# A hybrid encoder block on one core: the order of the later input projections

## The chip, the cores and the metric

The kernel runs on one core of a Trainium2 chip. The metric is the device time of one execution in microseconds. The core has five engines that each work through a queue of their own: TensorE (PE in the profile; its weight loads are PEld), VectorE (DVE), ScalarE (ACT), GpSimd (POOL) and SyncE (SP), which here only issues DMAs.

## The reference

One layer of an encoder on 1024 tokens of width 1024, all in float32. Both mixers read one input projection:

```python
xn = _rmsnorm(h, norm_mix_w[l])
proj = xn @ w_in[l]                       # columns: q_a, k_a, v_a, qkv_g, z_g, a_g, b_g
attn = _windowed_gqa(q_a, k_a, v_a, ...)  # 8 query heads on 2 key/value heads, window +-128, bias table, sink
gdn  = _gdn_mixer(qkv_g, z_g, a_g, b_g, ...)
h = h + jnp.concatenate([attn, gdn], axis=-1) @ w_out[l]
h = h + jnp.square(jax.nn.relu(_rmsnorm(h, norm_ffn_w[l]) @ w_ffn_in[l])) @ w_ffn_out[l]
return _rmsnorm(h, norm_final_w)
```

The second mixer, a gated delta rule in both directions, works on four heads of width 128. Its q, k and v pass a convolution over 5 tokens and Silu; in chunks it needs the inverse of a triangular matrix (I + A), where A comes from the Gram products of k, and then a scan over the chunks. Its output is normalised and multiplied by Silu(z), the gate.

## The kernel before

Products in full precision are made of three matmuls on a high and a low part of each operand (`mm3`, L124 to L126; the parts come from `split`, a cast on ScalarE, L119, and a subtraction on GpSimd, L120). A product of 128 weight columns with 512 tokens is `gemm`: 8 x 3 matmuls into one PSUM bank of the tag `psA`, of which there are four. `pair` makes four such products from 256 columns, in the order half 0 of both blocks, then half 1 of both; whoever uses `pair` copies each bank out.

Keys and queries of the delta rule are projected first. Then two streams of instructions are woven together by weights. The first is the rest of the input projection: v of the delta rule (`proj_conv`), the gate (`proj_z`), and keys, values and queries of attention (`proj_attn`). The second makes the inverses: `prep` (Gram products per chunk, L631 and L633, decay by Exp on ScalarE, L643, scaling on VectorE, L647 and L655, copies of diagonal blocks, L652, stores to memory `atd` and `pd`), `eliminate` for each direction (31 steps of two VectorE instructions, L675 and L677), `diag_blocks` (VectorE transposes, L686 and L687) and `invert` for the first two of four pairs of chunks (small matmuls L720, L730, L734, L753, L761 with ScalarE copies L714, L723, L744, L755 and memsets on GpSimd, L710, between them). After that, `bias_table` loads four tables of attention's bias (L529), and attention is woven with the other inverses and the scan.

How each projection leaves PSUM:
- v of the delta rule: a ScalarE copy (L394) into a tile of 1028 tokens, on VectorE a scaling (L373) and four multiply-adds (L375) per head, Silu (L377), transposes on PE (L409), a VectorE multiplication (L449) and a store (L450). The tiles and the results lie in buffers of the tag `sc`, of which there are four; `eliminate(1)` and `diag_blocks(1)` use the same tag for their matrices.
- the gate: Silu on ScalarE (L458) and a store `zd` (L459).
- keys and values of attention: a VectorE copy (L476), for keys two DMAs that swap halves, casts and a subtraction; for values a transpose on PE and a copy (L488).
- queries: on VectorE a scaling (L494), on ScalarE a cast (L495), on GpSimd a subtraction (L496), four stores `qad` (L500). `query` (L594) is a DMA on GpSimd's queue that loads a block of queries back. The first two such loads were issued from inside the loop over query products.

The order of the instructions on each engine is set when the kernel is built, by a scheduler that goes by the order in which the code issues them, by buffers that come free, and by its own estimate of times; at run time each engine takes its queue in that order. ScalarE computes Exp and Silu from tables that it loads when the function changes (rows ACT_TABLE_LOAD in the profile).

Of the kernel before, what the change touches and what calls it, by code (L numbers as in the profile page):

```python
# [29 lines left out]
C_AQ, C_AK, C_AV = 0, 512, 640  # L30
C_GQ, C_GK, C_GV, C_Z, C_AB = 768, 1280, 1792, 2304, 2816
# [23 lines left out]
def weave(*streams):  # L55

    live = [[0.0, i, g, w] for i, (g, w) in enumerate(streams)]
    while live:
        s = min(live, key=lambda e: (e[0], e[1]))
        try:  # L60
            v = next(s[2])
            s[0] += v / s[3]
            yield v
        except StopIteration:
            live.remove(s)


def run(gen):
    for _ in gen:
        pass  # L70


def chain(*gens):
    for g in gens:
        yield from g


class Block:
# [380 lines left out]
                nc.sync.dma_start(out=self.zd[2 * p + i, :, half * HALF:(half + 1) * HALF], in_=z)  # L459
                yield 5.2  # L460

    def proj_attn(self):


        nc = self.nc
        w = self.io["w_in"][0]
        raws = self.load_w(self.w_cols(w, C_AK, 256))
        lo, up = slice(0, 64), slice(64, 128)
        self.kh, self.kl = [self.pg(dt=F32R) for _ in range(2)], [self.pg(dt=F32R) for _ in range(2)]
        for v, o in enumerate((up, lo)):  # L470
            nc.vector.tensor_copy(out=self.kl[v][o, :], in_=self.zero[o, :].to_broadcast([64, SEQ]))
        self.va = self.pg((P, NT, P))
        for i, half, ps in self.pair(raws):
            tok = slice(half * HALF, (half + 1) * HALF)
            t = self.pt()
            nc.vector.tensor_copy(out=t, in_=ps)  # L476
            if i == 0:
                swap = self.pt()
                nc.sync.dma_start(out=swap[up, :], in_=t[lo, :])
                nc.sync.dma_start(out=swap[lo, :], in_=t[up, :])  # L480
                for v, (r, o) in enumerate(((lo, up), (up, lo))):
                    nc.scalar.copy(out=self.kh[v][r, tok], in_=t[r, :])
                    nc.scalar.copy(out=self.kh[v][o, tok], in_=swap[o, :])
                    nc.gpsimd.tensor_tensor(out=self.kl[v][r, tok], in0=t[r, :], in1=self.kh[v][r, tok].bitcast(F32),
                                            op=ALU.subtract)
            else:
                pv = self.transposed(t, 0)
                nc.vector.tensor_copy(out=self.va[:, 4 * half:4 * half + 4, :], in_=pv)  # L488
            yield 5.2
        for kv in range(2):  # L490
            raws = self.load_w(self.w_cols(w, C_AQ + 256 * kv, 256))
            for i, half, ps in self.pair(raws):
                q, qh = self.pt(), self.pt(dt=F32R)
                nc.vector.tensor_scalar(out=q, in0=ps, scalar1=0.125, scalar2=None, op0=ALU.mult)  # L494
                nc.scalar.copy(out=qh, in_=q)  # L495
                nc.gpsimd.tensor_tensor(out=q, in0=q, in1=qh.bitcast(F32), op=ALU.subtract)  # L496
                for part, t in enumerate((qh.bitcast(F32), q)):
                    o = 64 * (kv ^ part)
                    for g in range(2):
                        nc.sync.dma_start(out=self.qad[kv, 2 * i + g, o:o + 64, half * HALF:(half + 1) * HALF],  # L500
                                          in_=t[64 * g:64 * g + 64, :])
                if i == 1 and half == 0:
                    self.qs.append(self.query(0, kv))
                yield 5.2


# [747 lines left out]
    def phases(self):  # L1254
        nc = self.nc
        w = self.io["w_in"][0]
# [9 lines left out]
        for half in range(2):  # L1266
# [5 lines left out]
            else:  # L1272
# [11 lines left out]
        tt = [[None] * 4, [None] * 4]  # L1284
        self.ct, self.ctt = [None, None], [None, None]
        self.kc, self.qc = [None] * 4, [None] * 4
        self.qs = []
        self.wo, self.hnt, self.scanned, self.summed, self.rows = [{}, {}], [None, None], set(), [], {}
        run(weave((chain(self.proj_conv(C_GV, "v"), self.proj_z(), self.proj_attn()), 145.0),
                  (chain(self.prep(), self.eliminate(0), self.diag_blocks(0), self.eliminate(1), self.diag_blocks(1),  # L1290
                         self.invert(tt, (0, 1))), 100.0)))
        self.bias_table()

        self.X = {n: [] for n in ("B11", "B21", "B22", "N1", "T2", "T3", "N4")}
        cols, rest = {}, {}
# [82 lines left out]
```

## Time and profile before

| | us |
|---|---|
| median of 3 runs (lowest, highest) | 1255.21 (1253.97, 1259.02) |
| the profiled execution, its own time | 1255.02 |
| its span, from the first to the last instruction | 1253.3 |
| TensorE busy | 1191.6 |
| VectorE busy | 854.9 |
| ScalarE busy | 621.4 |
| GpSimd busy | 580.3 |

The mean granted TensorE clock is 0.983 of full speed. All times of instructions are microseconds from the start of the span. Matmuls overlap in the pipeline, so a row of 0.40 us can follow the one before it after 0.23 us. A row with a bracket shows how long the engine was idle before the instruction and what ended that; the releaser is inferred, and can be a neighbour of the true one. Groups by line show the count, busy us, the mean ns of one, and the idle time before them.

### The profile page before, as it was taken

To read this page: it belongs to the slowest core of one execution; us is meant where nothing else is said; L and a number is where in the kernel's file an instruction comes from. 1 tells how busy PE (TensorE), PEld (TensorE's weight loads), DVE (VectorE), ACT (ScalarE), POOL (GpSimd) and SP (SyncE) were. 2 spreads that over 40 slices of the span, in tenths; PEclk is the share of its full clock that TensorE was granted. 3 is DMA by queue.
4 is the path that set the end of the run, shared out by engine and by line. 5 is a ranking of instruction groups with operands and counts; after the bars stand their busy time and mean duration, and the time that the engine had idled before them with its cause. 6 is when DMAs were issued, how large, how long until landed. Compare 5 with 4: busy or idle time off the path is not lost.

```text
span 1253.3 us, 18527 instructions
## 1 busy us (share of the span) xinstructions
PE 1191.6 (95%) x6482; PEld 967.2 (77%) x6482; DVE 854.9 (68%) x1528; ACT 621.4 (50%) x1347; POOL 580.3 (46%) x488
## 2 busy tenths in 40 slices
PE   7999999899789989998999999999999999999997
PEld 5778777677568868877788888888777888888885
DVE  5667667982389986676655454544668797886976
ACT  6455688335485752125464554545545434444343
POOL 5354211362432433144573534535445665655595
PEclk9999999899889999998999999999999999999999
DMA  7134344441956678122234344443678624434323
GB/s 239 52 121 133 101 171 140 139 126 40 223 168 158 190 216 296 60 84 85 84 131 159 132 151 143 154 159 134 223 280 280 223 85 167 151 121 148 95 90 135
DMA packets 121630, 187.62 MB, mean 150 GB/s; under 512 B 11043, under 2 KB 64416, under 8 KB 121537
## 3 DMA queue, kind: packets, MB, share of 16 engines
q1 hardware_dynamic: 96708, 152.58, 37.9%
q10 hardware_dynamic: 16381, 29.67, 6.3%
q0 software_dynamic: 8448, 4.20, 1.9%
q8 instruction: 51, 0.84, 0.3%
q14 instruction: 42, 0.34, 0.1%
HBM read 122.39 MB, written 63.49 MB: 148 GB/s over the span
## 4 chain that ended last, share of the span: by engine, by line
PE 49%; DVE 6%; DMA 3%; issue 2%; POOL 1%; ACT 1%; ACTq 0%; POOLq 0%; DVEq 0%; SPq 0%
PE psA L124 8%; PE psA L125 8%; PE psA L126 8%; PE psB L126 7%; PE psB L125 7%; PE psB L124 7%; DMA pg<-sd 3%; PE psB L797 2%; DVE pg L1154 1%; DVE pt L1163 1%; DVE wr L1166 1%; PE psB L209 1%; DVE pg L1199 1%; DMA sd<-pt 0%; DVE wr L1161 0%
## 5 line engine op out<-in xcount | busy, mean ns | idle before, releaser
L124 PE MATMUL psA<-pg,wh 128*128 128x512 f32 x416 | 167.6, 404 | 2.1 <-ACT pt L458 2.1
L126 PE MATMUL psA<-pg,wl 128*128 128x512 f32 x416 | 166.9, 401 | 0.0
L125 PE MATMUL psA<-pg,wh 128*128 128x512 f32 x416 | 166.5, 400 | 0.0
L120 POOL TENSOR_TENSOR wl<-wr,wh 128x512 fp32r<-128x512 f32 x44 | 70.2, 1618 | 154.0 <-ACT wh L119 153.9
L1154 DVE TENSOR_TENSOR pg<-pg 128x512 fp32r<-128x512 f32 x112 | 122.7, 1127 | 18.8 <-ACT pg L1153 18.6
L120 POOL TENSOR_TENSOR wh<-wr,wh 128x512 fp32r<-128x512 f32 x32 | 47.9, 1518 | 131.5 <-ACT wh L119 131.5
L1071 ACT ACTIVATE pt<-pt 128x512 f32<-128x512 f32 x64 | 40.4, 632 | 122.7 <-DVE pt L1061 122.7
L125 PE MATMUL psA<-pg,pg 128*128 128x512 f32 x256 | 99.7, 391 | 0.5 <-POOL pg L120 0.5
L124 PE MATMUL psA<-pg,pg 128*128 128x512 f32 x256 | 99.0, 391 | 1.0 <-DVE pg L1199 1.0
L126 PE MATMUL psA<-pg,pg 128*128 128x512 f32 x256 | 99.7, 389 | 0.0
L120 POOL TENSOR_TENSOR pg<-wr,pg 128x512 fp32r<-128x512 f32 x48 | 73.4, 1560 | 51.0 <-ACT pg L119 51.0
L124 PEld LDWEIGHTS psA<-pg,wh 128*128 128x128 f32 x416 | 79.2, 190 | 21.3 <-ACT pt L458 2.4
L125 PEld LDWEIGHTS psA<-pg,wh 128*128 128x128 f32 x416 | 79.3, 191 | 19.7 <-issue 0.9
L126 PEld LDWEIGHTS psA<-pg,wl 128*128 128x128 f32 x416 | 79.1, 190 | 18.6
L1153 ACT CAST pg<-pg 128x512 fp32r<-128x512 f32 x112 | 67.2, 620 | 41.3 <-DMA pg<-sd 31.0
L126 PE MATMUL psB<-pg,pg 128*128 128x512 f32 x192 | 75.0, 390 | 1.3 <-DVE pg L1154 1.3
L125 PE MATMUL psB<-pg,pg 128*128 128x512 f32 x192 | 75.0, 391 | 0.8 <-POOL pg L120 0.7
L124 PE MATMUL psB<-pg,pg 128*128 128x512 f32 x192 | 74.7, 390 | 0.4 <-ACT pg L1153 0.4
L119 ACT CAST wh<-wr 128x512 fp32r<-128x512 f32 x76 | 43.6, 623 | 45.5 <-PE psA L125 24.8
L1061 DVE TENSOR_TENSOR pt<-psB,pt 128x512 f32<-128x512 f32 x39 | 26.9, 689 | 55.1 <-PE psB L126 30.1
L1061 DVE TENSOR_TENSOR pt<-psA,pt 128x512 f32<-128x512 f32 x39 | 26.8, 689 | 55.0 <-PE psA L126 39.5
L124 PEld LDWEIGHTS psA<-pg,pg 128*128 128x128 f32 x256 | 48.0, 188 | 12.6 <-DVE pg L1199 2.3
(385 smaller groups left out, 3307.7 us busy)
## 6 DMA issues: line engine op xcount, KB each, us to landing
sd<-pt ACTq DMA_DIRECT2D x112, 256.0 KB, 2.2
pg<-sd SPq DMA_DIRECT2D x112, 256.0 KB, 2.9
wr<-in_w_ffn_in SPq DMA_DIRECT2D x32, 512.0 KB, 3.8
wr<-in_w_in SPq DMA_DIRECT2D x22, 512.0 KB, 4.8
pg<-in_x SPq DMA_DIRECT2D x16, 512.0 KB, 5.4
wr<-in_w_ffn_out SPq DMA_DIRECT2D x16, 512.0 KB, 4.8
sc<-kvd SPq DMA_DIRECT2D x14, 512.0 KB, 4.1
kvd<-pt SPq DMA_DIRECT2D x16, 256.0 KB, 2.8
```

The source lines that it names most:

```text
L119: nc.scalar.copy(out=h, in_=raw)
L120: (eng or nc.gpsimd).tensor_tensor(out=l, in0=raw, in1=h.bitcast(F32), op=ALU.subtract)
L124: nc.tensor.matmul(ps, wh, xh, start=first, stop=False, skip_group_check=onto)
L125: nc.tensor.matmul(ps, wh, xl, start=False, stop=False, skip_group_check=onto)
L126: nc.tensor.matmul(ps, wl, xh, start=False, stop=last, skip_group_check=onto)
L209: self.nc.tensor.transpose(ps[:, i * P:(i + 1) * P], row[:, k * P:(k + 1) * P], self.ident)
L797: nc.tensor.matmul(ps[:, h - g.start, :], left(h), right[:, h, :], start=True, stop=True)
L1061: self.nc.vector.tensor_tensor(out=out, in0=in0, in1=in1, op=ALU.add)
L1071: self.nc.scalar.activation(out=c, in_=c, func=AF.Relu)
L1153: nc.scalar.copy(out=s[:, 0], in_=raw)
L1154: v.tensor_tensor(out=s[:, 1], in0=raw, in1=s[:, 0].bitcast(F32), op=ALU.subtract)
L1163: v.tensor_tensor(out=b["T2"], in0=b["B22"], in1=b["T1"], op=ALU.subtract)
```

## The change

The first stream is issued in another order: queries of attention, v of the delta rule, keys and values of attention, the gate. For this `proj_attn` is cut into `proj_kv` and `proj_queries`. The first two loads of query blocks leave the loop and follow `bias_table`. No instruction of another kind is added and none is taken out, apart from table loads.

```diff
-    def proj_attn(self):
-
+    def proj_kv(self):
...
             yield 5.2
+
+    def proj_queries(self):
+
+        nc = self.nc
         for kv in range(2):
-            raws = self.load_w(self.w_cols(w, C_AQ + 256 * kv, 256))
+            raws = self.load_w(self.w_cols(self.io["w_in"][0], C_AQ + 256 * kv, 256))
...
-                if i == 1 and half == 0:
-                    self.qs.append(self.query(0, kv))
                 yield 5.2
...
-        self.qs = []
...
-        run(weave((chain(self.proj_conv(C_GV, "v"), self.proj_z(), self.proj_attn()), 145.0),
+        run(weave((chain(self.proj_queries(), self.proj_conv(C_GV, "v"), self.proj_kv(), self.proj_z()), 145.0),
...
         self.bias_table()
+        self.qs = [self.query(0, kv) for kv in range(2)]
```

Lines behind the cut shift by one to three (L476 becomes L475, L488 L487, L494 L497, L496 L499, L500 L503; L631 becomes L632 and so on by one).

VectorE's queue before, at the copy of the first product of values (`psA_2442`, into `pt_2467`): it stands among the steps of the elimination (`sc_2231`, `sc_2233` are the matrices of direction 1, `pg_1921`, `pg_1923` those of direction 0).

```order
L677 TENSOR_TENSOR sc_2233<-sc_2233,pt_2236 128x10x22
L675 TENSOR_TENSOR pt_1926<-pg_1921,pg_1923 128x112
L675 TENSOR_TENSOR pt_2236<-sc_2231,sc_2233 128x207
L677 TENSOR_TENSOR pg_1923<-pg_1923,pt_1926 128x4x28
L476 COPY pt_2467<-psA_2442 128x512
L677 TENSOR_TENSOR sc_2233<-sc_2233,pt_2236 128x9x23
```

The same queue now, at the copies of the first products of keys and values (`psA_2436` keys of half 0, `psA_2490` values of half 0, `psA_2533` keys of half 1). `sc_2238` is the elimination's matrix of direction 1, `sc_2333` and `sc_2396` are the convolved v heads 2 and 3.

```order
L373 TENSOR_SCALAR sc_2333<-sc_2232,cols 128x1024
L678 TENSOR_TENSOR sc_2238<-sc_2238,pt_2241 128x31
L375 SCALAR_TENSOR_TENSOR sc_2333<-sc_2232,cols,sc_2333 128x1024 x4
L373 TENSOR_SCALAR sc_2396<-sc_2277,cols 128x1024
L375 SCALAR_TENSOR_TENSOR sc_2396<-sc_2277,cols,sc_2396 128x1024 x2
L449 TENSOR_TENSOR pt_2345<-psB_2340,irk 128x512
L449 TENSOR_TENSOR pt_2353<-psB_2348,irk 128x512
L687 STREAM_TRANSPOSE sc_2530<-sc_2238 128x1024
L375 SCALAR_TENSOR_TENSOR sc_2396<-sc_2277,cols,sc_2396 128x1024 x2
L688 STREAM_TRANSPOSE sc_2529<-sc_2238 128x1024
L449 TENSOR_TENSOR pt_2408<-psB_2403,irk 128x512
L449 TENSOR_TENSOR pt_2416<-psB_2411,irk 128x512
```

The three copies out of PSUM (`pt_2461`, `pt_2515`, `pt_2558`) come directly behind these rows. They moved from among the elimination's steps to behind its last one (L678, the second row) and behind two convolutions.

TensorE's queue now, where the last product of values (`psA_2683`) ends and the first of the gate (`psA_2764`) begins; before, the first product of queries followed the last product of values directly.

```order
L126 MATMUL psA_2683<-pg_427,wl_2485 128x512
L409 MATMUL psB_2340<-ident,sc_2333 128x128 x4
L409 MATMUL psB_2348<-ident,sc_2333 128x128 x4
L409 MATMUL psB_2403<-ident,sc_2396 128x128 x4
L409 MATMUL psB_2411<-ident,sc_2396 128x128 x4
L124 MATMUL psA_2764<-pg_218,wh_2758 128x512
```

The transposes of v heads 2 and 3 moved in between, and `psA_2764` takes the bank of the fourth product before it, `psA_2436`.

GpSimd's queue before, in the last part of the query products (`pg_2756` and `pg_3229` are tiles that `invert` clears, `pt_2904` and `pt_3096` the first query blocks):

```order
L496 TENSOR_TENSOR pt_2895<-pt_2895,pt_2896 128x512
L594 DMA pt_2904<-qad 128x4x128
L710 MEMSET pg_2756 128x1024
L496 TENSOR_TENSOR pt_2969<-pt_2969,pt_2970 128x512
L496 TENSOR_TENSOR pt_3003<-pt_3003,pt_3004 128x512
L496 TENSOR_TENSOR pt_3047<-pt_3047,pt_3048 128x512
L496 TENSOR_TENSOR pt_3087<-pt_3087,pt_3088 128x512
L594 DMA pt_3096<-qad 128x4x128
L710 MEMSET pg_3229 128x1024
```

And now:

```order
L711 MEMSET pg_2798 128x1024
L711 MEMSET pg_3229 128x1024
L595 DMA pt_3182<-qad 128x4x128
L595 DMA pt_3184<-qad 128x4x128
L595 DMA pt_3221<-qad 128x4x128
```

The loads of query blocks moved behind the memsets of `invert`.

## The prediction

> **What bounds the kernel now.** I read the page first, then the wait list of TensorE, then the timeline and the busy time by stretch around the second half of the input projection, the only part whose order changes.
>
> ```profile
> PE 1191.6 (95%) x6482; PEld 967.2 (77%) x6482; DVE 854.9 (68%) x1528; ACT 621.4 (50%) x1347; POOL 580.3 (46%) x488
> ```
>
> TensorE (PE) is busy for 1191.6 of 1253.3 us, and each engine works through its own queue in order. A reordering cannot take work off PE; it can only change what PE waits for. So the question is how long PE stands still between the first Gram product of `prep` and the first attention score, before and after. Stretches before (columns: stretch, length, busy PE, PE weight loads, VectorE, ScalarE, GpSimd, granted clock, DMA share, GB/s):
>
> ```profile
> 217.50:224.60 7.10, 2.56 (x16) 1.60 (x16) 5.61 (x13) 6.98 (x17) 3.72 (x6) 0.92 0.83 280
> 223.80:280.30 56.50, 55.67 (x230) 44.36 (x230) 50.47 (x139) 16.42 (x29) 25.22 (x18) 0.94 0.37 115
> 281.00:336.00 55.00, 49.50 (x611) 39.83 (x612) 14.54 (x26) 24.36 (x40) 15.42 (x15) 0.97 0.42 103
> 336.00:360.00 24.00, 17.36 (x313) 14.70 (x315) 16.88 (x62) 19.88 (x50) 11.61 (x14) 0.72 0.71 191
> 360.00:460.00 100.00, 94.24 (x844) 77.31 (x833) 94.46 (x314) 66.31 (x192) 32.50 (x31) 1.00 0.68 190
> ```
>
> PE loses 7.10 - 2.56 = 4.5 us at 217 to 224, 5.5 us at 281 to 336 and 6.6 us at 336 to 360. From 360 to 460 VectorE (94.46 of 100) sets the pace. The individual waits (start, duration, instruction, idle time before it and its releaser):
>
> ```profile
> 141.19 1.05 PE L631 MATMUL psB<-pg 128*128 128x128 f32 x8
> 221.83 0.66 PE L409 MATMUL psB<-ident,sc 128*128 128x128 f32 x4 [1.73 <-DVE pt L655]
> 224.63 0.79 PE L124 MATMUL psA<-pg,wh 128*128 128x512 f32 x1 [2.15 <-ACT pt L458]
> 225.22 0.63 PE L125 MATMUL psA<-pg,wh 128*128 128x512 f32 x1
> 225.65 0.63 PE L126 MATMUL psA<-pg,wl 128*128 128x512 f32 x1
> 233.84 0.40 PE L125 MATMUL psA<-pg,wh 128*128 128x512 f32 x1
> 239.44 0.40 PE L125 MATMUL psA<-pg,wh 128*128 128x512 f32 x1
> 272.52 0.40 PE L124 MATMUL psA<-pg,wh 128*128 128x512 f32 x1
> 322.12 1.68 PE L761 MATMUL psB<-pg,pt 64*64 64x64 f32 x32 [4.36 <-ACT pt L755]
> 335.97 0.29 PE L544 MATMUL psA<-pg,pt 128*128 128x256 f32 x1
> 339.60 0.28 PE L720 MATMUL psB<-pg,pg 32*32 32x32 f32 x2 [2.12 <-DMA pg<-atd]
> ```
>
> The two L125 rows at 233.84 and 239.44 are 24 matmuls, one product of a 128-column weight block, apart: 5.60 us, or 0.233 us each. After the wait at 224 the pitch is 0.43 us (225.22 to 225.65): the granted clock had halved. Row 141.19 is the last place where both kernels have issued the same PE work; 272.52 is where the first query product begins before, and 335.97 the first attention score.
>
> **The change, step 1: what it takes away.** Before, the convolution of v runs while `prep` runs, and ScalarE swaps its function table between Silu and Exp:
>
> ```profile
> L643 ACT ACT_TABLE_LOAD x5 | 6.4, 1283 | 3.3 <-issue 3.2
> L377 ACT ACT_TABLE_LOAD x4 | 5.1, 1283 | 0.1
> L458 ACT ACT_TABLE_LOAD x1 | 1.3, 1283 | 0.0
> ```
>
> In the new order Exp is loaded once for `prep` and Silu once for v and the gate: two loads for ten in this stretch, 8 x 1.283 = 10.3 us less on ScalarE, which was 98% busy (6.98 of 7.10) where PE stood. So the 4.5 us at 217 and the half-clock matmuls after it (about 13 x 0.2 = 2.6 us) should go. What covers `prep` instead is query work: per product one 0.6 us cast on ScalarE and one scaling on VectorE, and 4 small DMAs on SP, between SP's stores of `prep`.
>
> **Step 2: the prefetches.** The first query tile was loaded on GpSimd's queue in the middle of the query products, and the load must wait until the stores of queries behind it have landed. The chain before:
>
> ```profile
> 316.94 1.00 POOL L594 DMA_DIRECT2D pt<-qad  x1 [3.89 <-DMA pg<-biasd]
> 317.95 0.97 POOL L710 MEMSET pg<- 128x1024 f32 x1
> 318.95 2.51 ACT L714 COPY pg<-sc 32x256 f32<-32x256 f32 x4 [7.32 <-POOL pg L710]
> 321.48 0.59 ACT L755 COPY pt<-psB 128x512 f32<-128x512 f32 x1
> ```
>
> GpSimd's next instruction, a memset, is late, then the ScalarE copies behind it, then PE's L761 by 4.36 us. Now both loads stand behind the bias table and the memsets, when the queries have long been stored. The 4.36 us goes, and so do most of the PE waits at 337 to 343. SP issues the bias and block loads between 8 gate stores instead of 32 query stores, which costs nothing as PE has 45 us of gate products over it. Gone in all: some 17 us that before stand between 141 and 343.
>
> **Step 3: what is late next.** VectorE's queue now holds, between the last `prep` tile and the first copy of a key/value product out of PSUM (L475), the whole elimination of both directions and all four v convolutions, the last two behind the elimination because their work buffers (`sc`, 4 of them) are held by it. The first gate product needs the PSUM bank that this copy frees, and ahead of it in PE's queue stand the transposes of v heads 2 and 3. VectorE prices before:
>
> ```profile
> L375 DVE SCALAR_TENSOR_TENSOR sc<-sc,cols,sc 128x1024 f32<-128x1024 f32 x16 | 22.7, 1426 | 0.4
> L373 DVE TENSOR_SCALAR sc<-sc,cols 128x1024 f32<-128x1024 f32 x4 | 3.5, 883 | 3.4 <-ACT sc L394 3.4
> L449 DVE TENSOR_TENSOR pt<-psB,irk 128x512 f32<-128x512 f32 x4 | 2.6, 680 | 1.9 <-PE psB L409 1.9
> L664 DVE STREAM_TRANSPOSE pg<-pg 128x1024 f32<-128x1024 f32 x1 | 1.2, 1245 | 0.6 <-ACT pg L652 0.6
> L476 DVE COPY pt<-psA 128x512 f32<-128x512 f32 x3 | 2.0, 680 | 5.4 <-PE psA L126 5.4
> L488 DVE COPY pg<-psB 128x512 f32<-128x512 f32 x1 | 0.7, 676 | 0.0
> L687 DVE STREAM_TRANSPOSE sc<-sc 128x1024 f32<-128x1024 f32 x1 | 1.9, 1873 | 0.0
> ```
>
> The stretch 223.80 to 280.30 holds the elimination with its transposes, four of the eight L449 and the zero casts: 50.47 us busy. Less the copies that now come later (2.0 + 0.7), plus v's convolutions (22.7 + 3.5 = 26.2), the other four L449 (2.6), two L664 (2.4) and the rest of L687 (1.8): 80.8 us, in one queue.
>
> PE in the new order: from 141.19 to the end of `prep`, 176 matmuls (41.1 us) and eight chunks of about 2.6 us (21 us), so 203. VectorE's stretch starts when ScalarE has copied the last diagonal blocks, some 5 us later (before it was 4.7), at 208, and ends at 289. PE meanwhile has ten products (56 us), 1.8 us of v transposes and a wait of about 1.6 us for the last query's bank: it is done at 263. It then waits until 290: **some 26 us**, in place of the 17 of steps 1 and 2, and starts again at half clock (3.4 us lost, as after 224).
>
> From the first gate product to the first score before: 335.97 - 272.52 = 63.5 us, of which 4.36 + 1.6 are waits and 1.5 half clock; 56 remain. The new order puts the third block's L720 and L730 (2.2 us) ahead of the score, PE now awaits three sets of ScalarE copies with no product of its own in between (twice L755, 0.59 us and the way there and back, 2 us in all; then the last gate's Silu and the third block's copies, for which I take the like four of 2.51 us and 1.5 us more: 6 us together), and there is the half clock: 56 + 2.2 + 6 + 3.4 = 67.6, so the first score comes at 290 + 67 = 357 against 336: 21 us late.
>
> **Step 4: what comes back.** Before, VectorE idles 24 - 16.88 = 7.1 us at 336 to 360, while PE waits for blocks and queries. After, those are there and the third block is already partly done. I take 6 us back (bounds: 0, and 7.1 plus the 5.5 that VectorE idles until 460). Net 21 - 6 = **15 us slower**. From the profiled execution's own 1255.0 us (1253.3 span and 1.7 around it; the median of runs, 1255.21, is the same within 0.2) this gives 1270.
>
> Bounds of the stretch: with no interference from GpSimd the convolution step is nearer its 1.27 us than 1.426 (2.5 us less), and four elimination steps that took 1.3 us instead of 0.25 would take 4.2 less: 74 us. Above, GpSimd's weight subtractions decide:
>
> ```profile
> 244.84 10.23 POOL L120 TENSOR_TENSOR wl<-wr,wh 128x512 fp32r<-128x512 f32 x4 [20.53 <-ACT wh L119]
> 263.52 0.24 DVE L677 TENSOR_TENSOR pg<-pg,pt 128x87 f32<-128x87 f32 x1
> 274.62 1.34 DVE L677 TENSOR_TENSOR sc<-sc,pt 128x87 f32<-128x87 f32 x1
> ```
>
> The same instruction took 0.24 us alone and 1.34 us beside GpSimd, while in dense VectorE work GpSimd was the one held up (10.23 us for four). I take the sum as it was measured, with the four slow ones in it. The Trainium skill, "SBUF — State Buffer", section "Who interferes with whom", has VectorE instructions with two SBUF inputs share a read port with GpSimd instructions that read SBUF, and whichever issues second blocks for the whole instruction. The rows above agree with it both ways. By the rows the sum stays at 80.8 us; with GpSimd first each time the page would make it, as an estimate, about 90.
>
> **The rivals.**
> - *GpSimd holds up VectorE more* (slower still). Eight subtractions of v's second pair, keys and gate fall into the new stretch. If each blocks one VectorE step by 1.1 us, 9 us more: 1279. For it: row 274.62; against: row 244.84. Chance 0.17. The Trainium skill's page named above would give this case wherever GpSimd issues first.
> - *The delay is absorbed.* If attention and the scan have slack that PE's start does not show, all of the 7.1 + 5.5 us comes back and the stretch is at its lower bound: 21 - 12.6 - 6.7 = 2, so 1257. Against it: VectorE is 94% busy from 360 on. Chance 0.16.
> - *PE never waits for VectorE* (faster). If the v convolutions and elimination end before PE has finished the key/value products, only steps 1 and 2 remain: 4.5 + 2.6 + 4.4 and 1 us of half clock go, 1243. It decides at a stretch of 55 us instead of 80.8. Against it is the order of the queues; for it, only that I may have an instruction's price wrong by a third. Chance 0.08.
> - The forecast: 0.59.
>
> **How the numbers follow.** A measurement of this kernel tells about 0.5% (6 us) from no change. Slower: the forecast, of which I put 0.02 within 0.5%, and the first rival: 0.74. Same: 0.18. Faster: 0.08. The range reaches from the absorbed case to the upper bound of the first rival and 5 us of PE waits in `prep` that I cannot see: 1255 to 1284. The forecast's own is 1262 to 1278.
>
> **What would show it.** No PE wait for the gate's first bank, nor for L409 before the Gram products end, and two table loads until 260 (step 1). No 4 us PE wait on L756 (the old L755) for a late memset (step 2). PE idle for 20 to 30 us near 263 to 290, released by VectorE or by the Silu of v heads 2 and 3, and half clock after it (step 3). First score near 357, and from there less VectorE idle time than before (step 4). I am wrong if VectorE reaches the key/value copies before about 270, or if the end moves by less than half of what the first score moves.

## The result and the profile after

| | before | after |
|---|---|---|
| median of 4 runs, us (lowest, highest) | 1255.86 (1253.97, 1259.02) | 1292.62 (1288.14, 1296.42) |
| ratio of the times, 95% interval | | 1.028 (1.0257 to 1.0303) |
| profiled execution, its span | 1253.3 | 1286.4 (its own time 1288.14) |
| mean granted clock | 0.983 | 0.969 |
| first attention score, first and last matmul of the scan, us | 336.0, 374.1, 564.7 | 366.0, 400.6, 591.6 |
| from there to the end of the span | 688.6 | 694.8 |

The change costs 2.8%. The direction was forecast, the size was not: 15 us were forecast, 33.1 are in the profiled pair of spans and 37 in the medians. The sum below is made against the spans. Of the runs in this document one was slow: it belongs to e12_one_store, took 1729.22 us at a granted clock of 0.65, and is in that run's median but not in its ratio.

The page after, busy time of each engine:

```profile
PE 1198.0 (93%) x6482; PEld 972.5 (76%) x6482; DVE 854.0 (66%) x1528; ACT 610.6 (47%) x1339; POOL 573.9 (45%) x488
```

The work is the same, so the 33 us are waiting and half clock. Where they lie, by stretches of the changed kernel (stretch, length, busy PE, PE weight loads, VectorE, ScalarE, GpSimd, clock, DMA share, GB/s):

```profile
141.00:203.00 62.00, 62.00 (x337) 51.12 (x337) 28.99 (x79) 48.76 (x137) 17.84 (x14) 1.00 0.70 212
203.00:262.00 59.00, 58.73 (x261) 47.31 (x259) 57.19 (x124) 19.21 (x39) 20.96 (x20) 1.00 0.29 90
262.00:295.60 33.60, 4.05 (x18) 3.16 (x17) 31.79 (x52) 3.23 (x5) 2.94 (x2) 0.58 0.07 21
295.60:366.00 70.40, 64.80 (x808) 51.27 (x808) 10.81 (x21) 37.00 (x61) 19.80 (x24) 0.91 0.51 144
366.00:400.60 34.60, 28.85 (x390) 22.39 (x384) 27.82 (x100) 25.37 (x70) 9.68 (x11) 0.80 0.36 101
400.60:591.60 191.00, 180.70 (x1165) 152.04 (x1162) 152.71 (x463) 81.30 (x243) 62.40 (x52) 0.99 0.55 169
591.60:640.00 48.40, 40.70 (x177) 33.81 (x176) 23.08 (x39) 17.89 (x37) 15.20 (x20) 0.86 0.26 87
```

Up to 262 PE has work for all but 0.3 us and runs at full clock: the stall of 4.5 us that before lay at 217 is gone. Then it works 4.05 of 33.6 us while VectorE works 31.79 of them. The single rows on PE:

```profile
261.69 0.40 PE L126 MATMUL psA<-pg,wl 128*128 128x512 f32 x1
283.76 1.97 PE L409 MATMUL psB<-ident,sc 128*128 128x128 f32 x8 [21.67 <-ACT sc L377]
292.23 1.97 PE L409 MATMUL psB<-ident,sc 128*128 128x128 f32 x8 [6.50 <-ACT sc L377]
295.58 0.79 PE L124 MATMUL psA<-pg,wh 128*128 128x512 f32 x1 [1.38 <-DVE pt L475]
296.17 0.63 PE L125 MATMUL psA<-pg,wh 128*128 128x512 f32 x1
296.60 0.63 PE L126 MATMUL psA<-pg,wl 128*128 128x512 f32 x1
329.11 1.97 PE L762 MATMUL psB<-pg,pt 64*64 64x64 f32 x32 [2.94 <-ACT pt L756]
```

PE stands first for the transposes of v heads 2 and 3 (L409, whose Silu L377 waits for VectorE's convolution), and only 1.38 us of the 29.6 for the bank that the key copy L475 frees. The gate then starts at half clock (0.43 us from 296.17 to 296.60). The last row is the wait that step 2 was to take away; 2.94 us of its 4.36 are left.

The last stretch, from the scan's last matmul on, in the old kernel:

```profile
564.70:613.10 48.40, 44.81 (x207) 37.26 (x207) 29.36 (x45) 20.53 (x41) 19.68 (x24) 0.93 0.29 99
```

PE gets 44.81 us of work done there before and 40.70 after, 300 us behind the change. The rows that end PE's longest wait in it (ScalarE, VectorE, PE of the changed kernel):

```profile
608.91 0.31 ACT L901 ACTIVATE scr<-pg 128x128 f32<-128x128 f32 x1
610.96 0.69 ACT L967 ACTIVATE pg<-psB,cols 128x512 f32<-128x512 f32 x1 [1.64 <-PE psB L209]
613.25 0.30 ACT L901 ACTIVATE scr<-pg 128x128 f32<-128x128 f32 x1
619.63 0.68 DVE L908 TENSOR_TENSOR wr<-pg,sm 128x512 f32<-128x512 f32 x1
620.37 1.12 PE L911 MATMUL psA<-ident,wr 128*128 128x128 f32 x4 [4.12 <-DVE wr L908]
```

The scan's last chunk is squared by four ScalarE instructions of 0.3 us. Before, three stood in a row and one behind one copy L966; now two of them stand behind copies L967 that wait for PE. VectorE's small steps behind the Squares moved too: before, L902 to L905 stood almost together (585.13 to 586.38), and now the same steps, L903 to L906, are spread among other instructions (613.87, 615.58, 616.25, 617.63). So L908 is late, and the transposes L911 behind it.

### The profile page after: what moved, and what is told of

It is laid out like the page before. It is cut to its first block, busy times and chain, and to the rows that moved or that the text cites. A ratio compares the mean times of both kernels' runs of the same rounds, so it can differ in the third digit from the quotient of the medians.

```text
span 1286.4 us, 18510 instructions
## 1 busy us (share of the span) xinstructions
PE 1198.0 (93%) x6482; PEld 972.5 (76%) x6482; DVE 854.0 (66%) x1528; ACT 610.6 (47%) x1339; POOL 573.9 (45%) x488
## 4 chain that ended last, share of the span: by engine, by line
PE 48%; DVE 6%; issue 3%; DMA 2%; POOL 2%; ACT 1%; POOLq 0%; ACTq 0%; DVEq 0%
PE psA L124 8%; PE psA L125 8%; PE psA L126 8%; PE psB L124 7%; PE psB L125 7%; PE psB L126 7%; DMA pg<-sd 2%; PE psB L798 2%; POOL pg L120 1%; DVE pt L1164 1%; DVE wr L1167 1%; DVE pg L1200 1%; DVE pg L215 0%; DVE wr L1162 0%; DVE pg L1155 0%
## 5 line engine op out<-in xcount | busy, mean ns | idle before, releaser
L120 POOL TENSOR_TENSOR wl<-wr,wh 128x512 fp32r<-128x512 f32 x44 | 64.6, 1491 | 99.3 <-ACT wh L119 96.2
L1062 DVE TENSOR_TENSOR pt<-psB,pt 128x512 f32<-128x512 f32 x39 | 26.9, 689 | 54.0 <-PE psB L126 29.0
```

What stands on the lines that cost most here:

```text
L120: (eng or nc.gpsimd).tensor_tensor(out=l, in0=raw, in1=h.bitcast(F32), op=ALU.subtract)
L1062: self.nc.vector.tensor_tensor(out=out, in0=in0, in1=in1, op=ALU.add)
```

## The experiments

The table gives each run's median and its ratio to the old kernel, run beside it on one chip, and from its profile the first score, the scan's first matmul, and the time from the scan's last matmul to the end.

| run | median us | ratio (95%) | first score | scan | rest |
|---|---|---|---|---|---|
| changed kernel | 1292.62 | 1.0280 (1.0257 to 1.0303) | 366.0 | 400.6 | 694.8 |
| e1_tail | 1285.79 | 1.0215 (1.0186 to 1.0243) | 363.4 | 399.3 | 689.7 |
| e2_no_low | 1281.17 | 1.0178 (1.0146 to 1.0209) | 355.7 | 391.6 | 696.8 |
| e3_gate_third | 1287.53 | 1.0223 (1.0198 to 1.0247) | 357.4 | 394.7 | 698.3 |
| e4_defer | 1274.38 | 1.0128 (1.0100 to 1.0156) | 348.3 | 383.8 | 694.4 |
| e9_no_taps | 1274.31 | 1.0146 (1.0122 to 1.0170) | 347.7 | 384.2 | 694.3 |
| e5_prefetch | 1266.00 | 1.0083 (1.0057 to 1.0109) | 343.2 | 376.0 | 695.0 |
| e6_prefetch_tail | 1259.10 | 1.0023 (1.0010 to 1.0036) | 342.0 | 374.9 | 691.9 |
| e15_two_queues | 1257.38 | 1.0007 (0.9994 to 1.0020) | 338.8 | 375.0 | 688.1 |
| e16_old_two_queues | 1260.44 | 1.0027 (1.0013 to 1.0041) | 336.6 | 374.6 | 691.5 |
| e7_conv_early | 1272.89 | 1.0130 (1.0109 to 1.0152) | 354.4 | 387.8 | 689.7 |
| e8_conv_early_kv | 1270.79 | 1.0116 (1.0094 to 1.0137) | 351.3 | 384.9 | 690.2 |
| e10_v_q_kv_z | 1270.42 | 1.0112 (1.0093 to 1.0131) | 350.9 | 384.4 | 691.9 |
| e11_v_q_z_kv | 1265.16 | 1.0071 (1.0053 to 1.0089) | 342.6 | 379.9 | 688.5 |
| e17_vqzk_two_queues | 1266.46 | 1.0079 (1.0058 to 1.0099) | 343.2 | 383.3 | 690.8 |

**The far end.** In the changed kernel:

```diff
-            nc.scalar.activation(out=scr, in_=o[:, h, :], func=AF.Square, ...)
+            nc.scalar.activation(out=mix[:, h, :] if c == 0 else scr, in_=o[:, h, :], func=AF.Square, ...)
```

> The new order of projections, with one edit far behind it: the four Squares of the last gated chunk of the second scan write different slices instead of one scratch tile, so that the scheduler puts the four of them in one row on ScalarE, ahead of the first copies of the second norm half. In the trace of the changed kernel the last two Squares stand behind such copies, and PE waits 4.12 us at 620 for L911 and runs at half clock after it; all that follows is 33.3 us late against 27 at the end of the scan. Theory A (the schedule of the whole program is made anew, and this place costs some 6 us): the wait goes and the time falls by 5 to 7 us, to 1286 or so where the changed kernel has 1292.6. Rival B (the late end comes from the scan itself, and ScalarE's order there is only a mark of it): the time stays within 2 us of the changed kernel's.

Theory A held: in the trace of this run the four Squares stand in one row on ScalarE (610.27 to 611.15). PE's waits for L911 in all, in the changed kernel and then in this one (us in total, times, longest):

```profile
PE psA L911 <- DVE wr L908: 5.0, 3, 4.1
```

```profile
PE psA L911 <- DVE wr L908: 1.0, 2, 0.7
```

The four Squares wrote one scratch tile; with a slice each the scheduler puts them in a row. In the table every kernel with this edit has a rest of 688 to 692 us, and every one without it but the old kernel 694 to 698. So some 5 to 7 us of the loss (5.1 behind the scan in the traces, 6.8 in the medians) are a scheduler's choice that the change only set off, 300 us behind it. In the old order, where three Squares stood in a row already, the edit brings nothing (e16_old_two_queues: 691.5 against 688.6).

**GpSimd's reads.** The changed kernel without the low halves of the weights of v, keys, values and gate, for which GpSimd writes zeros:

```diff
-        (eng or nc.gpsimd).tensor_tensor(out=l, in0=raw, in1=h.bitcast(F32), op=ALU.subtract)
+        nc.gpsimd.memset(l.bitcast(F32), 0.0) if self.nolow else (eng or nc.gpsimd).tensor_tensor(...)
```

> The new order, with the low halves of the weights of v, keys, values and gate left out: GpSimd writes zeros there instead of subtracting, and reads no SBUF for it (the result is less exact). The order of instructions on every engine is the same. In the changed kernel VectorE needed 87 us from the last prep tile to the first copy of a key/value product (208 to 294.8), and twelve of its steps that take 0.2 to 0.4 us elsewhere took 1.1 to 1.5 there, each beside a subtraction on GpSimd. Theory A (each subtraction on GpSimd holds up one VectorE step by some 1.1 us): the twelve are short again, the stretch is 74 to 76 us, PE's wait ahead of L409 and L475 is 11 to 13 us shorter, and the time falls by 10 to 13, to about 1281. Rival B (the slow steps have another cause): stretch 87 us and no change in time beyond 2 us.

Theory A held: key copy at 284.5 instead of 294.8, time as named. The elimination's four groups in one and the same stretch of the span (207.80 to 294.80): changed kernel, old kernel, this run.

```profile
L678 DVE TENSOR_TENSOR pg<-pg,pt 128x31 f32<-128x31 f32 (+15 forms) x31 | 16.2, 522 | 0.2
L676 DVE TENSOR_TENSOR pt<-pg,pg 128x31 f32<-128x31 f32 (+15 forms) x31 | 13.4, 431 | 0.2
L678 DVE TENSOR_TENSOR sc<-sc,pt 128x31 f32<-128x31 f32 (+15 forms) x31 | 12.6, 405 | 0.3
L676 DVE TENSOR_TENSOR pt<-sc,sc 128x31 f32<-128x31 f32 (+15 forms) x31 | 10.3, 334 | 0.4
```

```profile
L677 DVE TENSOR_TENSOR sc<-sc,pt 128x31 f32<-128x31 f32 (+15 forms) x31 | 12.9, 417 | 0.1
L675 DVE TENSOR_TENSOR pt<-sc,sc 128x31 f32<-128x31 f32 (+15 forms) x31 | 12.4, 400 | 0.1
L677 DVE TENSOR_TENSOR pg<-pg,pt 128x31 f32<-128x31 f32 (+15 forms) x31 | 11.4, 369 | 0.1
L675 DVE TENSOR_TENSOR pt<-pg,pg 128x31 f32<-128x31 f32 (+15 forms) x31 | 10.3, 332 | 0.2
```

```profile
L676 DVE TENSOR_TENSOR pt<-pg,pg 128x31 f32<-128x31 f32 (+15 forms) x31 | 11.7, 376 | 0.2
L676 DVE TENSOR_TENSOR pt<-sc,sc 128x31 f32<-128x31 f32 (+15 forms) x31 | 10.6, 343 | 0.4
L678 DVE TENSOR_TENSOR sc<-sc,pt 128x31 f32<-128x31 f32 (+15 forms) x31 | 10.6, 342 | 0.3
L678 DVE TENSOR_TENSOR pg<-pg,pt 128x31 f32<-128x31 f32 (+15 forms) x31 | 10.5, 340 | 0.2
```

The 124 steps sum to 52.5, 47.0 and 43.4 us: against this run the new order loses 9.1 us and the old one 3.6. With 1.0 us of the convolution (L375: 21.5 us, here 20.5) the 9.1 are nearly all of the 10.3 by which the key copy comes earlier. One place of the changed kernel, VectorE and then GpSimd:

```profile
210.32 0.21 DVE L678 TENSOR_TENSOR pg<-pg,pt 128x31 f32<-128x31 f32 x1
210.56 1.18 DVE L676 TENSOR_TENSOR pt<-pg,pg 128x60 f32<-128x60 f32 x1
211.78 1.22 DVE L678 TENSOR_TENSOR pg<-pg,pt 128x60 f32<-128x60 f32 x1
213.03 1.23 DVE L676 TENSOR_TENSOR pt<-pg,pg 128x87 f32<-128x87 f32 x1
```

```profile
210.34 2.58 POOL L120 TENSOR_TENSOR wl<-wr,wh 128x512 fp32r<-128x512 f32 x2 [2.66 <-ACT wh L119]
212.88 1.28 POOL L499 TENSOR_TENSOR pt<-pt,pt 128x512 f32<-128x512 f32 x1
```

Three subtractions, three steps of 1.2 us where such a step takes 0.2. Both inputs of these steps lie in SBUF. The Trainium skill, "SBUF — State Buffer", section "Who interferes with whom", has a VectorE instruction with two SBUF inputs contend with a GpSimd instruction that reads SBUF, not with one that only writes it; the run agrees, since beside the memsets one step of the elimination is long (212.34, beside a subtraction of L499 that is left) where eleven were.

**What PE stands for.** Order queries, v, gate, keys and values:

```diff
-chain(self.proj_queries(), self.proj_conv(C_GV, "v"), self.proj_kv(), self.proj_z())
+chain(self.proj_queries(), self.proj_conv(C_GV, "v"), self.proj_z(), self.proj_kv())
```

> Order queries, v, gate, keys and values: the gate's eight products, which need nothing from VectorE, come where the key/value products were. PE's row of instructions still has the transposes of v's third and fourth head (L409) at the same place, behind the twelfth product after prep, now ahead of the fifth gate product or so. Theory A (PE stands for these transposes, whose convolution VectorE has not done, at a place that the scheduler chose by its own times): PE stops at about 262 as before for 20 to 28 us, and the time is 1283 to 1295. Rival B (PE stands for the copy of the first key product out of PSUM, L475): the gate's products fill the gap, and the time falls to 1255 to 1265.

Theory A held, with a longer stop than the 20 to 28 us named: PE stands for 22.30 and 9.10 us at the same L409, though the key copies now come only at 336. So the transposes are enough for the wait, without the key copy. (The score is 8.6 us earlier than in the changed kernel; the far end takes 3.5 us of it back.)

Next, the same order with v's late transposes behind all products, and the results of v heads 2 and 3 in buffers that the elimination does not hold:

```diff
-                    out = None if kind == "v" else self.pg()
+                    out = None if kind == "v" and h < 2 else self.pg()
...
-                    getattr(self, "head_" + kind)(h, out)
+                    (self.later.append((h, out)) if kind == "v" and h > 1 else getattr(self, "head_" + kind)(h, out))
...
+chain(self.proj_queries(), self.proj_conv(C_GV, "v"), self.proj_z(), self.proj_kv(), self.rest_v())
```

> Order queries, v, gate, keys and values, and the transposes of v's third and fourth head (with their scaling and stores) behind all of them; the convolution results of these two heads stand in other buffers for it, so that VectorE does their convolution ahead of the second elimination's end. Nothing that PE has to do between the end of prep and the key/value products now needs the end of VectorE's stretch, except the first block products (L721) of the inverse. Theory A (the wait was for a place in the queue, not for the amount of VectorE's work): PE runs through from 203 to about 305 with waits of 0 to 8 us, the first attention score comes at 320 to 330 (336 in the old order, 366 in the new), and the time is 1240 to 1254. Rival B (the 87 us of VectorE work itself sets the pace, and PE waits for it at the block products or the copies instead): first score at 345 or later, time 1265 or more.

Theory A failed and rival B held. PE's longest waits between 262 and 300:

```profile
PE psB L721 <- DVE sc L688: 10.1, 1, 10.1
PE psB L721 <- issue: 3.1, 1, 3.1
```

Now PE waits for the inverse's block products, because VectorE, with the same amount of work (83.58 us busy from 207.00 to 292.40, 82.87 in the changed kernel), gives the last diagonal transposes (L688) only at 290.53. Moving the waiting instruction won 18 of 37 us, not all: the rest of PE's wait is for VectorE's work itself, which is too late.

The new order, with four of the five taps of v's convolution left out:

```diff
-        for j in (0, 1, 3, 4):
+        for j in (0, 1, 3, 4) if ct < 8 else ():
```

> The new order, with four of the five taps of v's convolution left out: 16 of VectorE's instructions (L375, 21.5 us in the changed kernel between 208 and 294.8) are gone, PE's and GpSimd's work is the same, and PE's row still has the transposes of v's third and fourth head and the copies' banks at the same place. Theory A (PE stands until VectorE's row is done, so that its sum counts one for one): the first copy of a key product comes at 270 to 275 instead of 294.8, PE stands for 10 to 14 us instead of 31, and the time falls by 20 to 25 us, to 1268 to 1273. Rival B (v's results wait for the second elimination, whose buffers they need, and not for the convolution's own length): the copy comes at 285 or later, and the time falls by less than 10.

Rival B is out, and theory A's mechanism held with less than it named: 21.5 us of VectorE's work are gone, PE stands for 9.2 us at L409 and 2.7 for L475 instead of 29.6 in all, the key copy comes 17.0 us earlier (277.8; 270 to 275 was expected), the first score 18.3, and the time falls by 18 (20 to 25 was expected). So some 17 of the 21.5 us counted, not one for one.

**Step 2 alone.** The old order with the query loads behind the bias table; then with the row of Squares too; then with half of the query stores on ScalarE's queue:

```diff
-                if i == 1 and half == 0:
-                    self.qs.append(self.query(0, kv))
...
+        self.qs = [self.query(0, kv) for kv in range(2)]
```

```diff
-                        nc.sync.dma_start(out=self.qad[...], in_=...)
+                        (nc.scalar if part else nc.sync).dma_start(out=self.qad[...], in_=...)
```

> The old order (v, gate, keys and values, queries), with one part of the change done alone: the two first query loads are issued behind the bias table instead of amid the query products. Theory A (step 2 of the prediction holds by itself): GpSimd's memset L711 is no longer behind the load, PE's wait of 4.36 us ahead of L762 at 322 goes and so does part of the 6.6 us at 336 to 360; first score at about 331 and 4 to 8 us less in all, near 1249 where the old order has 1256. Rival B (the wait moves to the load itself, which is now issued later and awaited by the first score): no change within 2 us.

> As the run before, and the four last Squares of the second scan in one row on ScalarE (as in the first experiment). Theory A: the old order has three of the four in a row, so little is to be had there: 0 to 3 us less than without, if the load alone moved one of them back. Rival B (the row of Squares was worth its 7 us only because all that follows was already late): no difference at all.

> The old order with the query loads behind the bias table and the row of Squares, and the stores of the low halves of the queries issued on ScalarE's queue instead of SP's (16 of 32; the shapes of the stores are the first ones, 64 rows of 2 KB). Theory A (SP's issue time, 300 to 343, made the moved loads useless): SP comes to the third block's loads some 8 us earlier, PE's 10.3 us at 342 shrink to 0 to 3, first score at 332 to 338, time 1246 to 1254. Rival B (the block load waits for its buffer): the wait stays at 8 us or more, time 1256 to 1261.

> The old kernel with the same two queues for the query stores and the row of Squares; the query loads stay amid the query products. Theory A: the stores behind which GpSimd's load stands land earlier, PE's 4.36 us ahead of L761 goes or halves, and the waits at 336 to 360 shrink: 1248 to 1254. Rival B (the load stands behind the bias loads, which SP issues after the stores, and ScalarE's 16 issues of about 0.5 us delay its casts): 1255 to 1260.

The first run was slower than the old kernel, which neither of its theories had. The wait ahead of L762 went (1.0 us left in all), and this came (PE, then SP, of that run):

```profile
342.97 0.28 PE L721 MATMUL psB<-pg,pg 32*32 32x32 f32 x2 [10.74 <-DMA pg<-atd]
```

```profile
322.62 13.53 SPq L503 DMA_DIRECT2D qad<-pt  x20
336.19 1.07 SPq L530 DMA_DIRECT2D pg<-biasd  x2
337.35 0.38 SPq L708 DMA_DIRECT2D pg<-atd  x1
```

The scheduler put the third block's first products ahead of the first score, and their load stands on SP behind query stores. About 6 of the 8.9 us were the far end again (rest 695.0); the row of Squares took the time down to 1259.10, by 6.9 us where its theories had 0 to 3. With half of the stores off SP the block loads come 8 us earlier and the longest wait for one is 2.0 us, as theory A had it, but the time is the old kernel's (theory A had 1246 to 1254): the scan starts at 375.0 against 374.1. So the 4.36 us that step 2 takes away do not reach the scan; what follows them was not ready earlier. With the loads where they were, two queues leave the wait (4.3 us ahead of L761, so theory A failed) and take 1260.44, 3 us more than with the loads moved. That difference does not come ahead of the scan, which starts at 374.6 there; its cause was not separated.

**Orders with v first.** All with the row of Squares; the first two do half of v's convolution beside `prep` and its Silu and transposes later, the others keep `proj_conv` whole and change the `chain` alone.

```diff
-        nc.scalar.activation(out=acc, in_=acc, func=AF.Silu)
+        ct >= 8 or nc.scalar.activation(out=acc, in_=acc, func=AF.Silu)
```

> Order v, queries, gate, keys and values, with v's Silu, transposes and stores behind all of them (and the row of Squares). VectorE does half of v's convolution beside prep, where it is idle for some 35 of 67 us in the changed kernel; ScalarE swaps its table no more than in the changed kernel, as no Silu stands in prep; no transposes of v stand ahead of the gate. Theory A (what counts is how much of VectorE's work lies between the end of prep and the last diagonal blocks of the inverse): that stretch is some 70 us instead of 87, PE waits for at most 8 us at the block products, first score at 328 to 342, time 1238 to 1256. Rival B (any order that starts with v pays for it on ScalarE in prep as the old one did, and the late transposes pay again before the scan): 1256 to 1270.

> Order v, queries, then v's Silu, transposes and stores, keys and values, the gate last (and the row of Squares). As the run before, but Silu may fall beside prep (three table swaps), the transposes of v stand at two places in PE's row, the second ahead of the last query products, and the gate is again last ahead of the first score. Theory A: PE waits for the second set of transposes as in the changed kernel but shorter, since half of the convolution is done earlier: some 10 to 15 us, first score at 340 to 350, time 1255 to 1268. Rival B (the place of the transposes does not count as long as VectorE has less to do): as the run before within 3 us.

> Order v, queries, keys and values, gate last (and the row of Squares of the first experiment): the queries ahead of the keys and the gate as in the new order, but v's convolution beside prep as in the old one. Up to the end of prep (217) PE's row is the old one, with the wait of some 4 us for ScalarE and its tables. The query stores stand on SP between 225 and 280 instead of 290 to 343, where they held up the block loads (10.3 us in the run with the loads moved). Theory A (of the new order only v's place costs; queries ahead of the gate are a gain): first score at 328 to 338 and 1244 to 1254. Rival B (the key copies again stand on VectorE behind the elimination and the query scalings, and PE waits for the bank): PE stands 8 us or more ahead of the first gate products, first score at 343 or later, time 1258 or more.

> Order v, queries, gate, keys and values last (and the row of Squares). As the run before, but nothing that the gate needs stands behind the elimination on VectorE. Theory A: PE runs through the gate without a wait for VectorE, but the keys are made last and their copies, swaps and transposes stand between the last product and the first score: first score 4 to 8 us later than in the run before, time 1248 to 1260. Rival B (keys last cost nothing, as the inverse's products cover them): within 2 us of the run before, or below it.

> Order v, queries, gate, keys and values last, with the row of Squares and the two queues. With all stores on SP PE stood 6.1 us at 277 for a block load behind them, and the time was 1265. Theory A: that wait is 0 to 2 us, first score at 334 to 338, time 1255 to 1261. Rival B (the load waits for buffers): 1263 to 1267.

Theory A failed in all five, to the slow side. The first lies beyond its rival B as well (1256 to 1270); the other four lie where their rivals B had them, but not always for the reason named. In e10_v_q_kv_z PE stands 4.19 us for the key copy L475 at 273.85 and 1.94 us for a gate's Silu, where rival B had 8 or more ahead of the first gate products. In the last, rival B had the block load wait for buffers. There the load's wait went, and PE stood at the same place for VectorE's elimination (L721 in e11_v_q_z_kv, then in e17_vqzk_two_queues):

```profile
277.32 0.28 PE L721 MATMUL psB<-pg,pg 32*32 32x32 f32 x2 [6.12 <-DMA pg<-atd]
276.81 0.28 PE L721 MATMUL psB<-pg,pg 32*32 32x32 f32 x2 [6.22 <-DVE sc L678]
```

All five are faster than the changed kernel and slower than the old one. No single wait explains it: the first has waits of 5.1 us (VectorE's query scaling L497), 5.0 (L721), 4.5 in three (L762), 3.0 and 2.5. Why each is worth what it is was not separated.

**One store for two.** Each query tile stored by one DMA of 128 rows, in three kernels (the old order with the loads moved, the old kernel, the order v, queries, gate, keys; all with the row of Squares):

```diff
-                    for g in range(2):
-                        nc.sync.dma_start(out=self.qad[kv, 2 * i + g, o:o + 64, ...], in_=t[64 * g:64 * g + 64, :])
+                    nc.sync.dma_start(out=self.qad[kv, 2 * i:2 * i + 2, o:o + 64, ...], in_=t)
```

> The old order with the query loads behind the bias table and the row of Squares, and each of the 16 query tiles stored by one DMA of 128 rows instead of two of 64: SP issues 16 stores between 290 and 343 instead of 32. Without this PE stood 10.3 us at 342 for the block load (L721 behind L708), while SP was busy issuing query stores and bias loads from 300 to 343 at some 0.6 us each. Theory A (SP's issue time is what made the moved loads useless): SP comes to the block loads 8 to 10 us earlier, the wait is 0 to 3 us, first score at 332 to 338, time 1246 to 1254. Rival B (the block load waits for its buffer or its data, not for SP): the wait stays at 8 us or more and the time at 1257 to 1261.

> The old kernel, with the query stores one DMA instead of two and the row of Squares, nothing moved: the query loads stand where they stood, amid the query products. Theory A: the loads' wait for the stores behind which they stand is shorter by some 2 us, so PE's 4.36 us ahead of L761 and its waits at 336 to 360 shrink; 2 to 6 us less than the old kernel, 1250 to 1254. Rival B (the wait is one for the DMAs' landing, which takes as long for one store of twice the size): within 2 us of the old kernel.

> Order v, queries, gate, keys and values last, with the row of Squares and one store per query tile. In the same order with two stores PE stood 6.1 us at 277 for the block load, behind query stores on SP, and 4.6 us at 227 for VectorE's scaling of the first query product. Theory A: the 6.1 us and the half clock after it go, first score at 334 to 338, time 1255 to 1260. Rival B (the block load there waits for the diagonal blocks or its buffers): first score at 341 to 344, time 1263 to 1267.

1306.39, 1307.39 and 1309.09 us (ratios 1.0374, 1.0393 and 1.0404): 4% slower, which no theory had; the runs measured the store and not SP. SP's queue and a stretch in which little but these stores runs, in the second of them:

```profile
332.74 29.40 SPq L499 DMA_DIRECT2D qad<-pt  x7
```

```profile
336.00:360.00 24.00, 9.71 (x45) 7.82 (x43) 2.41 (x8) 3.89 (x6) 1.58 (x2) 0.75 0.13 52
```

Seven stores of 256 KB held SP for 29.4 us and moved 52 GB/s at 13% of the DMA engines. The Trainium skill, "DMA: Bandwidth & Descriptors", section "Why a DMA increments its semaphore by 16 and not by 1", splits a copy over the largest number of engines, at most 16, that divides the slowest dimension of both sides. Here one side's slowest dimension is the pair of blocks, so 2 of 16 engines, which is 12.5%. The share of 0.13 in the row agrees.

## Why the prediction was wrong in size

The forecast of the profiled span was +15; +33.1 came. Its own steps add up to the difference:

| step | forecast | measured | off by |
|---|---|---|---|
| start of the gate | 290 | 295.6 | +5.6 |
| from there to the first score | 67 | 70.4 | +3.4 |
| coming back until the scan's last matmul | 6 | 30.0 - 26.9 = 3.1 | +2.9 |
| behind the scan | 0 | 694.8 - 688.6 | +6.2 |

Together 18.1, and 15 + 18.1 = 33.1. The other 4 us of the medians lie between the profiled execution (1288.14) and the three others (1291.55 to 1296.42), which have no profile; that stays open.

- *Step 1* held: the wait at 217 is gone. Two table loads are all that ScalarE has between 141 and 345 (below). PE has no wait that a row shows above 0.3 us until 262, and was done with the values at 261.9 where 263 was forecast.

```profile
L644 ACT ACT_TABLE_LOAD x1 | 1.3, 1283 | 0.0
L377 ACT ACT_TABLE_LOAD x1 | 1.3, 1283 | 0.0
```

- *Step 2* failed as a gain. The memset was no longer behind a load, yet L762 waited 2.94 us of the 4.36, now behind ScalarE copies whose memset waits for a buffer that PE holds:

```profile
324.93 0.96 POOL L711 MEMSET wh<- 128x1024 f32 x1 [4.50 <-PE psA L125]
```

  In the old order the moved loads gained nothing on the old kernel, alone (1.0083), with the row of Squares (1.0023) or with two queues as well (1.0007). The prediction's "costs nothing" for SP was nearly right for the new order (1.4 us of waits for block loads), but in the old order SP's query stores are what the next wait is for.
- *Step 3* had the right mechanism, place and start (VectorE's row began at 207.87, forecast 208), and this is the term that was mis-sized first: 87 us instead of 80.8, inside the bounds of 74 to 90. I kept the slow steps of the old order (six of its rows are long, of which I counted four) and argued from row 244.84 that dense VectorE work holds GpSimd up instead. Both happen; the elimination was 5.5 us longer than before, eleven long steps for the subtractions beside it, which e2_no_low undoes. The first rival had this mechanism: it named 9 us more, and 5.5 came on top of the 3.6 that the old order loses already. It was nearer to the truth than the forecast, but its 1279 was too low as well. The convolution was cheaper than taken (21.5 + 3.0 for 26.2), and 2.2 us of the row were idle; 5.5 - 1.7 + 2.2 = 6.0 is the excess of the row, 87.0 - 80.8 = 6.2, within 0.2. The prediction named the key copy L475 as what the gate waits for and the transposes L409 as standing ahead; e3_gate_third shows that the transposes alone suffice.
- From the gate to the score 70.4 us passed where 67 were forecast. The waits were 5.6 us in all (70.40 - 64.80), no more than the 6 allowed. Half clock was taken once, but the granted clock was low twice: 0.55 from 295.6 to 302.0, and 0.67 from 326.0 to 334.0, behind the rest of the L762 wait. Ahead of the score PE also had 160 more small matmuls (1420 against 1260 from the first Gram product on), for which 2.2 us were taken. How the 3.4 us divide between these was not separated.
- *Step 4*: half of what was taken came back. The row from 360 to 460, on which it rests, has PE busy for 94.24 us beside VectorE's 94.46 and so did not show that VectorE alone sets the pace there. Absorption, the second rival, is ruled out for the changed kernel: of 30.0 us at the first score 26.5 are left at the scan's first matmul. It does hold where only the loads moved: 7.2 and 6.0 us at the score were 1.9 and 0.8 at the scan.
- *The missing step* is the far end: 6.2 us that the sum put at nothing without a reason. The sum ended at the scan; nothing in it allowed for a changed order of instructions that the diff does not touch. The same comparison of the two queues that served for the change would have shown two Squares behind the copies.

## What to carry to other kernels

Before moving work, find the cover that each part of it had: v's convolution ran on VectorE beside a stage that waited for ScalarE, and moved behind that stage some 17 of the 21.5 us of its multiply-adds were on the path. Where a scheduler orders the whole program, compare the old and new queues to the end, not only around the change. A stall that is removed is a gain only if what follows it is ready; ask for each what the next instruction then waits for.

## What the runs showed of the hardware

A VectorE step of 0.2 to 0.4 us, with both inputs in SBUF, took 0.89 to 1.55 us beside a GpSimd subtraction of 1.3 us, and did not beside GpSimd's memsets: 9.1 us in 124 steps. Half clock behind a stall lasted from 224.63 to 229.91 in the old kernel, after gaps of 1.73 and 2.15 us without a matmul, and from 295.58 to 301.29 in the new one. A store of 2 x 64 rows from one tile moved 52 GB/s, while the two stores of 64 rows it replaced landed 2.4 us after their issue (128 KB each, median).

```profile
qad<-pt SPq DMA_DIRECT2D x32, 128.0 KB, 2.4
```
